# Sums of weight quarters by DMAs that add while landing, in the seven-product down-projection of one transformer block

## The chip, the cores and the metric

The kernel runs on one core of a Trainium2 chip. The metric is the device time of one execution in microseconds, median of 3 runs. PE is the matmul engine (TensorE), PEld its weight loads, DVE is VectorE, ACT is ScalarE, POOL is GpSimd and SP is SyncE, which here only issues DMAs.

## What is computed

One block of a network with 512 positions and 2048 columns: attention of two kinds, then a feed-forward part. The change touches the last product of the feed-forward part:

```
h = rmsnorm(x, g_ffn_pre[l])
u = causal_depthwise_conv(h @ w_up[l], conv_w[l], conv_b[l])
gate, val = jnp.split(u, 2, axis=-1)
y = (jax.nn.gelu(gate, approximate=True) * val) @ w_down[l]
x = x + rmsnorm(y, g_ffn_post[l])
```

`w_up` is 2048 x 11264, `w_down` 5632 x 2048, all float32.

## The kernel before

**Splitting.** A float32 operand is split into two parts that TensorE can take: `hi`, which ACT makes by a cast, and `lo`, which DVE makes as operand minus `hi`. A product is three matmuls: hi x hi, hi x lo, lo x hi. For weights `w_parts` does this (L797 to L803): the cast is L800, tile `wh`, and the subtraction L802, tile `wl`. Both tiles have three buffers, so a split can be done at most two products ahead of the one that PE is at.

**Seven products.** Both feed-forward products are done by blocks of two by two with seven block products instead of eight. `sevenfold` (L809) makes the seven weight operands from four quarters w11, w12, w21, w22 of a block of weights: three of them are w11 + w12, w11 + w12 + w22 and w11 + w12 + w22 + w21, formed one from another in w11's own buffer, and one is w12 + w22, formed in w12's. The sums are made on DVE by `plus` (L805, L806, tile `wr`). The other side has seven operands too: g11, g5, g6, g7, g12, g3, g22.

**Down-projection.** The gelu output lies in memory in units (`g_dram`). Four units make a chunk (`FU = 4`), and there are five chunks. `g_sides` (L967) loads a chunk (L970, tile `gr`, 2 MiB) and makes the seven operands from it: casts on ACT (L964), subtractions on DVE (L965), and differences in place on DVE (L974, L976, L977, L981). For each chunk there are two groups, q = 0 and 1, of 512 of the 1024 columns of each half; each does seven products. So the stage has ten groups. `down_steps` (L994) loads a quarter, 1 MiB in 512 rows of 2 KB, from SP (L999; four buffers), and `down_product` (L983, matmuls L991) does 24 matmuls for a product. `add_to` moves the results from PSUM into accumulators (ACT L958 in the first chunk, DVE L960 afterwards).

**What sets the order.** The program makes the weight operand of a step two steps before its product is issued (the loop at the end of the function). A scheduler of the language then sets the order on each engine and picks the buffers; each engine and each queue runs its instructions in that order. The order of the products is m1, m5, m6, m7, m2, m3, m4, so the sides are used in the order g11, g5, g6, g7, g12, g3, g22. m1 and m2 share a PSUM bank pair (X), m5 and m3 another (D), m7 and m4 a third (C).

Of the kernel before, what the change touches and what calls it, by code (L numbers as in the profile page):

```python
# [9 lines left out]
F32 = mybir.dt.float32  # L10
# [4 lines left out]
ALU = mybir.AluOpType  # L15
# [4 lines left out]
P = 128  # L20
S = 512
NT = S // P
# [27 lines left out]
def hymba_block(ctx, tc, x, xT, positions, vecs, taps, w_in, w_uq, w_ukv, w_o, g_attn_post, w_up, w_down,  # L50
                g_ffn_post, out):
    nc = tc.nc
    te, ve, sc, po, sy = nc.tensor, nc.vector, nc.scalar, nc.gpsimd, nc.sync

    const = ctx.enter_context(tc.tile_pool(name="const", bufs=1))
    sm = ctx.enter_context(tc.tile_pool(name="sm", bufs=8))
# [11 lines left out]
    def bank():  # L68
        return pp.tile([P, 512], F32, tag="ps", name="ps")

    def f(t):
        return t.bitcast(F32)
# [40 lines left out]
        te.matmul(ps, ll, rh, start=False, stop=stop)  # L113

    def rstd_of(ss, n):
        m = sm.tile([P, NT], F32, tag="ms", name="ms")
        ve.tensor_scalar(m, ss, 1.0 / n, EPS, ALU.mult, ALU.add)
        r = sm.tile([P, NT], F32, tag="rs", name="rs", bufs=8)
        po.tensor_tensor(r, m, nhalf, ALU.pow)
        return r  # L120
# [433 lines left out]
    def mla_scores(hd):  # L554
        e = hd % 2
        (qh, ql), (kh, kl) = q_mla.pop(hd), k_mla.pop(hd)
        hs = slice(64 * e, 64 * e + 64)
        qr = rope_q[hd // 2][e]
        regs = all_scores([(qh, kh), (qh, kl), (ql, kh), (qr, krh), (qr[hs], krl[hs])], mlamask)
        mx = sm.tile([P, NT], F32, tag="mx", name="mx", bufs=2)  # L560
        for b, (z, c0, c1) in enumerate(regs):
            ve.tensor_reduce(mx[:, b:b + 1], z[:, c0:c1], AX.X, ALU.max)
        nb = sm.tile([P, NT], F32, tag="nb", name="nb", bufs=2)
        ve.tensor_tensor(nb, mx, nsq, ALU.mult)
        den = sm.tile([P, NT], F32, tag="den", name="den", bufs=2)
        p = [page(("om", "s")[e], 3) for _ in range(3)]
        for b, (z, c0, c1) in enumerate(regs):
            sc.activation(p[min(b, 2)][:, c0:c1], z[:, c0:c1], AF.Exp, bias=nb[:, b:b + 1], scale=sq_[:, b:b + 1],
                          accum_out=den[:, b:b + 1])
        rden = sm.tile([P, NT], F32, tag="rden", name="rden", bufs=2)  # L570
        ve.reciprocal(rden, den)
        for b, (z, c0, c1) in enumerate(regs):
            pt = p[min(b, 2)][:, c0:c1]
            po.tensor_scalar(pt, pt, rden[:, b:b + 1], 1.0, ALU.mult, ALU.mult)
        return aget(*p)
# [34 lines left out]
    a = {0: mla_scores(0), 1: mla_scores(1)}  # L610
# [111 lines left out]
    def cpage(name):  # L722
        return cp.tile([P, 8, 256], R32, name=name)

    a5, a6, a3 = ((cpage(n + "h"), cpage(n + "l")) for n in ("a5", "a6", "a3"))
    lo_half, hi_half = slice(0, 256), slice(256, 512)
    a11, a12 = ((act_hi[:, k, lo_half], act_lo[:, k, lo_half]) for k in (slice(0, 8), slice(8, 16)))
    a7, a22 = ((act_hi[:, k, hi_half], act_lo[:, k, hi_half]) for k in (slice(0, 8), slice(8, 16)))
# [68 lines left out]
    def w_parts(w):  # L797
        n, cols = w.shape[1], w.shape[2]
        hi = wq.tile([P, n, cols], R32, tag="wh", name="wh", bufs=3)
        sc.copy(hi, w)  # L800
        lo = wq.tile([P, n, cols], R32, tag="wl", name="wl", bufs=3)
        ve.tensor_tensor(lo, w, f(hi), ALU.subtract)  # L802
        return hi, lo  # L803

    def plus(w, v):  # L805
        ve.tensor_tensor(w, w, v, ALU.add)  # L806
        return w

    def sevenfold(quarter):  # L809

        def q(*a):
            w = quarter(*a)
            return w

        w = {}

        def p1():
            w[11] = q(0, 0)
            return w_parts(w[11])

        def p5():
            w[12] = q(0, 1)
            return w_parts(plus(w[11], w[12]))

        def p6():
            w[22] = q(1, 1)
            return w_parts(plus(w[11], w[22]))

        def p7():
            return w_parts(plus(w[12], w[22]))  # L830

        def p2():
            w[21] = q(1, 0)
            return w_parts(w[21])

        def p3():
            return w_parts(w[22])

        def p4():
            return w_parts(plus(w[11], w[21]))  # L840

        return p1, p5, p6, p7, p2, p3, p4
# [96 lines left out]
    FU = 4  # L939
# [4 lines left out]
    def open_down():  # L944
        some(len(later))
        for st in (tp_stack, cp_stack, hp_stack):
            st.close()
        d["ap"], ap_ = stacked("ap")
        d["lp"], d["lpool"] = stacked("lp")
        d["gp"], d["gpool"] = stacked("gp")  # L950
        d["acc"] = {n: {(t, q): ap_.tile([P, S], F32, name=f"acc{n}{t}{q}") for t in range(2) for q in range(2)}
                    for n in ("11", "u2", "22", "21", "12")}

    def add_to(n, q, bs, first, op=ALU.add):
        for t in range(2):
            a = d["acc"][n][t, q]
            if first:
                sc.copy(a, bs[t])  # L958
            else:
                ve.tensor_tensor(a, a, bs[t], op)  # L960
# [31 lines left out]
                              stop=k == FU - 1 and i == 2, skip_group_check=True)  # L992

    def down_steps(ch, q):  # L994
        def quarter(kh, nh):
            w = wq.tile([P, FU, S], F32, tag="wr", name="wr", bufs=4)
            c0 = nh * 1024 + q * 512
            rows = w_down[ch * FU * 2 * P:(ch + 1) * FU * 2 * P, c0:c0 + 512]
            sy.dma_start(w, rows.rearrange("(k j p) c -> p k j c", p=P, j=2)[:, :, kh, :])  # L999
            return w  # L1000

        first = ch == 0
        z = {}

        def m1(w):
            if q == 0:
                if first:
                    open_down()
                d["g"] = g_sides(ch)
            z["X"] = [bank(), bank()]  # L1010
            down_product(z["X"], w, d["g"][1], True)
            add_to("u2", q, z["X"], first)

        def m5(w):
            z["D"] = [bank(), bank()]
            down_product(z["D"], w, d["g"][5], True)
            add_to("22", q, z["D"], first)

        def m6(w):
            Y = [bank(), bank()]  # L1020
            down_product(Y, w, d["g"][6], True)
            add_to("u2", q, Y, False, ALU.subtract)

        def m7(w):
            z["C"] = [bank(), bank()]
            down_product(z["C"], w, d["g"][7], True)
            add_to("22", q, z["C"], False, ALU.subtract)

        def m2(w):
            down_product(z["X"], w, d["g"][2], False)  # L1030
            add_to("11", q, z["X"], first)

        def m3(w):
            down_product(z["D"], w, d["g"][3], False)
            add_to("12", q, z["D"], first)

        def m4(w):
            down_product(z["C"], w, d["g"][4], False)
            add_to("21", q, z["C"], first)

        return zip(sevenfold(quarter), (m1, m5, m6, m7, m2, m3, m4))

    y = {}

# [97 lines left out]
    for make, use in stream():  # L1142
        queue.append((use, make()))
        if len(queue) > 2:
            use, w = queue.pop(0)
# [59 lines left out]
```

## Time and profile before

| | us |
|---|---|
| median of 3 runs | 2146.44 (2141.97 to 2148.74) |
| the profiled execution | 2146.34 |
| its span, first to last instruction | 2144.6 |
| PE busy | 2037.9 (95%) |
| DVE busy | 1583.2 (74%) |
| ACT busy | 944.1 (44%) |
| POOL busy | 122.3 (6%) |

The profile is of one execution. Busy time is the time in which an engine runs an instruction; idle time is written beside the instruction that ended it, with what it waited for. The granted clock (PEclk) is the share of its full speed, 2.4 GHz, at which PE was let run in a stretch. The DMA share is the mean busy share of the sixteen DMA engines.

### The profile page before, as it was taken

Reading aid. Unit: us, or ns where it says so; the run is one execution under the profiler, and the core shown is the slowest. Engines: PE = TensorE matmul, PEld = TensorE weight load, DVE = VectorE, ACT = ScalarE, POOL = GpSimd, SP = SyncE. Lnnn points to the kernel's source line nnn. Section 1 sums busy time; section 2 is a strip of 40 time slices with the busy share of each in tenths; the row PEclk is TensorE's granted clock in tenths of the full one; section 3 lists DMA queues with packets and bytes.
Section 4 is the critical chain, followed back from the end, with each engine's and each line's share of the span. In section 5 each row is a group of like instructions: output and inputs, shape, how many; then the busy total and the mean of one; then the engine's idle time right before and its main releaser. Section 6 shows DMA issues by size and latency. Waiting matters only on the chain.

```text
span 2144.6 us, 30034 instructions
## 1 busy us (share of the span) xinstructions
PE 2037.9 (95%) x12784; PEld 1819.6 (85%) x12784; DVE 1583.2 (74%) x1491; ACT 944.1 (44%) x1124; POOL 122.3 (6%) x147
## 2 busy tenths in 40 slices
PE   8999999999999569999999999999997999999996
PEld 6788788877888569999999999999997778778785
DVE  7355355776233679989889889889889788999985
ACT  6243234455323854544444444444444543343332
POOL 0000001122021200000000000000000000000004
PEclk9999999999999779999999999999998999999998
DMA  8322322211422342342342432432434344324252
GB/s 273 98 71 77 98 76 63 76 33 60 143 93 79 118 150 96 110 156 90 126 140 89 139 127 89 155 111 96 155 105 147 128 138 138 118 79 160 96 175 99
DMA packets 179062, 245.16 MB, mean 114 GB/s; under 512 B 8176, under 2 KB 127088, under 8 KB 178928
## 3 DMA queue, kind: packets, MB, share of 16 engines
q1 hardware_dynamic: 174048, 227.04, 32.9%
q0 software_dynamic: 4448, 15.73, 1.8%
q8 instruction: 100, 1.64, 0.3%
q10 hardware_dynamic: 432, 0.47, 0.1%
q14 instruction: 34, 0.28, 0.0%
HBM read 223.29 MB, written 19.92 MB: 113 GB/s over the span
## 4 chain that ended last, share of the span: by engine, by line
PE 84%; DVE 8%; ACT 3%; DMA 2%; issue 1%; POOL 0%; DVEq 0%; ACTq 0%; POOLq 0%
PE ps L858 40%; PE ps L991 15%; PE ps L111 8%; PE ps L112 8%; PE ps L113 8%; PE ps L258 2%; DVE wr L806 1%; DVE wl L802 1%; DMA wr<-in_w_in_dram 1%; PE ps L234 1%; ACT wh L800 1%; DVE x L1094 1%; DVE t L438 1%; DVE wl L107 0%; ACT wh L105 0%
## 5 line engine op out<-in xcount | busy, mean ns | idle before, releaser
L800 ACT CAST wh<-wr 128x2048 fp32r<-128x2048 f32 x228 | 435.1, 1912 | 575.1 <-DVE wr L806 227.2
L802 DVE TENSOR_TENSOR wl<-wr,wh 128x2048 fp32r<-128x2048 f32 x228 | 519.1, 2288 | 111.5 <-ACT wh L800 111.1
L858 PE MATMUL ps<-act_hi,wh 128*128 128x256 f32 x1408 | 395.5, 281 | 15.0 <-ACT wh L800 15.0
L858 PE MATMUL ps<-act_hi,wl 128*128 128x256 f32 x1408 | 394.1, 280 | 1.5 <-DVE wl L802 1.5
L858 PE MATMUL ps<-act_lo,wh 128*128 128x256 f32 x1408 | 393.9, 280 | 0.0
L806 DVE TENSOR_TENSOR wr<-wr 128x2048 f32<-128x2048 f32 x128 | 292.6, 2286 | 1.3
L107 DVE TENSOR_TENSOR wl<-wr,wh 128x1024 fp32r<-128x1024 f32 (+2 forms) x105 | 128.1, 1220 | 210.4 <-ACT wh L105 210.3
L858 PEld LDWEIGHTS ps<-act_hi,wh 128*128 128x128 f32 x1408 | 265.5, 189 | 15.4 <-ACT wh L800 15.4
L858 PEld LDWEIGHTS ps<-act_hi,wl 128*128 128x128 f32 x1408 | 265.8, 189 | 1.8 <-DVE wl L802 1.8
L858 PEld LDWEIGHTS ps<-act_lo,wh 128*128 128x128 f32 x1408 | 264.5, 188 | 0.0
L105 ACT CAST wh<-wr 128x1024 fp32r<-128x1024 f32 (+2 forms) x105 | 108.0, 1028 | 234.3 <-PE ps L112 98.9
L111 PE MATMUL ps<-wh,act_hi 128*128 128x512 f32 (+1 forms) x448 | 163.9, 366 | 8.0 <-ACT act_hi L182 6.7
L112 PE MATMUL ps<-wl,act_hi 128*128 128x512 f32 (+1 forms) x448 | 163.3, 365 | 1.7 <-DVE wl L107 1.6
L113 PE MATMUL ps<-wh,act_lo 128*128 128x512 f32 (+1 forms) x448 | 162.9, 364 | 0.0
L111 PE MATMUL ps<-act_hi,wh 128*128 128x512 f32 x368 | 146.8, 399 | 0.0
L112 PE MATMUL ps<-act_lo,wh 128*128 128x512 f32 x368 | 145.7, 396 | 0.0
L113 PE MATMUL ps<-act_hi,wl 128*128 128x512 f32 x368 | 144.6, 393 | 0.0
L111 PEld LDWEIGHTS ps<-wh,act_hi 128*128 128x128 f32 x448 | 84.9, 190 | 22.6 <-ACT act_hi L182 6.7
L112 PEld LDWEIGHTS ps<-wl,act_hi 128*128 128x128 f32 x448 | 85.2, 190 | 16.9 <-DVE wl L107 2.4
L858 PE MATMUL ps<-a3h,wh 128*128 128x256 f32 x352 | 98.6, 280 | 0.0
L858 PE MATMUL ps<-a6h,wh 128*128 128x256 f32 x352 | 98.5, 280 | 0.0
L858 PE MATMUL ps<-a5h,wh 128*128 128x256 f32 x352 | 98.5, 280 | 0.0
(315 smaller groups left out, 4337.9 us busy)
## 6 DMA issues: line engine op xcount, KB each, us to landing
wr<-in_w_up_dram SPq DMA_DIRECT2D x88, 1024.0 KB, 5.4
wr<-in_w_down_dram SPq DMA_DIRECT2D x44, 1024.0 KB, 6.2
wr<-in_w_in_dram SPq DMA_DIRECT2D x59, 512.0 KB, 3.7
wr<-in_w_o_dram SPq DMA_DIRECT2D x32, 512.0 KB, 3.5
g_dram<-bg POOLq DMA_DIRECT2D x22, 512.0 KB, 5.2
gr<-g_dram SPq DMA_DIRECT2D x5, 2048.0 KB, 9.9
acc<-in_x_dram SPq DMA_DIRECT2D x16, 256.0 KB, 4.7
x<-in_x_dram SPq DMA_DIRECT2D x16, 256.0 KB, 5.4
```

Source lines behind the costliest of these rows:

```text
L105: sc.copy(hi, raw)
L107: ve.tensor_tensor(lo, raw, f(hi), ALU.subtract)
L111: te.matmul(ps, lh, rh, start=start, stop=False)
L112: te.matmul(ps, lh, rl, start=False, stop=False)
L113: te.matmul(ps, ll, rh, start=False, stop=stop)
L234: te.transpose(dst, a(b, j), ident)
L258: te.matmul(dst, q[:, b * P:(b + 1) * P], k[:, k0:S], start=i == 0, stop=False)
L800: sc.copy(hi, w)
L802: ve.tensor_tensor(lo, w, f(hi), ALU.subtract)
L806: ve.tensor_tensor(w, w, v, ALU.add)
L858: te.matmul(dst, l[:, k, ms], r[:, k, :], start=fresh and k == 0 and m == 0 and i == 0, stop=k == 7 and i == 2, skip_group_check=True)
L991: te.matmul(bs[t], l[:, k, ts_], r[:, k, :], start=fresh and k == 0 and i == 0, stop=k == FU - 1 and i == 2, skip_group_check=True)
```

## The change

In the down-projection, the four sums of a group are no longer made by DVE. GpSimd issues a DMA that reads the quarter to be added from memory and adds it to the buffer that already holds the other (`added`, with `accum_op`). w12 gets w22 added as soon as it has landed; w11 gets w12, w22 and w21 added in turn, each after ACT and DVE have split what was there before. SP still loads four quarters a group, and GpSimd issues four adds of 1 MiB each beside it. The products come in the order m1, m2, m5, m7, m6, m3, m4, so that between two products with w11's buffer another one lies. The up-projection keeps its sums on DVE. The memory for DMA descriptors grows from 1024 to 2048 bytes a partition, and one small tile gets 4 buffers instead of 8.

```diff
-        m = sm.tile([P, NT], F32, tag="ms", name="ms")
+        m = sm.tile([P, NT], F32, tag="ms", name="ms", bufs=4)
...
-    def sevenfold(quarter):
-
-        def q(*a):
-            w = quarter(*a)
-            return w
+    def sevenfold(quarter, added=None):
 
         w = {}
+        q = quarter
+
+        def a1():
+            w[11] = q(0, 0)
+            parts = w_parts(w[11])
+            w[12] = q(0, 1)
+            added(w[12], 1, 1)
+            added(w[11], 0, 1)
+            return parts
+
+        def a2():
+            w[21] = q(1, 0)
+            return w_parts(w[21])
+
+        def a5():
+            parts = w_parts(w[11])
+            added(w[11], 1, 1)
+            return parts
+
+        def a7():
+            return w_parts(w[12])
+
+        def a6():
+            parts = w_parts(w[11])
+            added(w[11], 1, 0)
+            return parts
+
+        def a3():
+            w[22] = q(1, 1)
+            return w_parts(w[22])
+
+        def a4():
+            return w_parts(w[11])
+
+        if added:
+            return a1, a2, a5, a7, a6, a3, a4
...
     def down_steps(ch, q):
+        def rows(kh, nh):
+            c0 = nh * 1024 + q * 512
+            r = w_down[ch * FU * 2 * P:(ch + 1) * FU * 2 * P, c0:c0 + 512]
+            return r.rearrange("(k j p) c -> p k j c", p=P, j=2)[:, :, kh, :]
+
         def quarter(kh, nh):
             w = wq.tile([P, FU, S], F32, tag="wr", name="wr", bufs=4)
...
+            sy.dma_start(w, rows(kh, nh))
             return w
+
+        def added(w, kh, nh):
+            po.dma_start(w, rows(kh, nh), accum_op=ALU.add)
...
-        return zip(sevenfold(quarter), (m1, m5, m6, m7, m2, m3, m4))
+        return zip(sevenfold(quarter, added), (m1, m2, m5, m7, m6, m3, m4))
...
-    nc = bacc.Bacc("TRN2", target_bir_lowering=False, num_devices=1, dynamic_dma_scratch_size=1024)
+    nc = bacc.Bacc("TRN2", target_bir_lowering=False, num_devices=1, dynamic_dma_scratch_size=2048)
```

What the change makes of the engines' order stands here at three places, all in the third chunk. First ACT, the casts of the weights in the group q = 1, with the last cast of the group ahead. Before (w11 is wr_16328, w12 wr_16360, w21 wr_16461, w22 wr_16393; wr_16064 is w11 of the group ahead):

```order
L800 CAST wh_16298<-wr_16064 128x2048
L800 CAST wh_16330<-wr_16328 128x2048
L800 CAST wh_16363<-wr_16328 128x2048
L964 CAST g11h_16632<-gr_16630 128x1024
L800 CAST wh_16396<-wr_16328 128x2048
L800 CAST wh_16429<-wr_16360 128x2048
L800 CAST wh_16463<-wr_16461 128x2048
L800 CAST wh_16495<-wr_16393 128x2048
L800 CAST wh_16528<-wr_16328 128x2048
```

Now (w11 is wr_16328, w21 wr_16364, w12 wr_16334, w22 wr_16492):

```order
L800 CAST wh_16296<-wr_16064 128x2048
L800 CAST wh_16330<-wr_16328 128x2048
L800 CAST wh_16366<-wr_16364 128x2048
L800 CAST wh_16396<-wr_16328 128x2048
L996 CAST g11h_16633<-gr_16631 128x1024
L800 CAST wh_16429<-wr_16334 128x2048
L996 CAST g12h_16656<-gr_16631 128x1024
L800 CAST wh_16459<-wr_16328 128x2048
L800 CAST wh_16494<-wr_16492 128x2048
L800 CAST wh_16526<-wr_16328 128x2048
```

The second cast of w11 has moved behind that of w21, and the third behind that of w12; the first still follows the last of the group ahead.

Second, the sums of a group: before on DVE, in the group q = 0 of that chunk (L806), between splits and accumulations:

```order
L806 TENSOR_TENSOR wr_16064<-wr_16064,wr_16096 128x2048
L806 TENSOR_TENSOR wr_16096<-wr_16096,wr_16129 128x2048
L802 TENSOR_TENSOR wl_16101<-wr_16064,wh_16099 128x2048
L960 TENSOR_TENSOR acc2101_15141<-acc2101_15141,ps_16005 128x512
L960 TENSOR_TENSOR acc2111_15143<-acc2111_15143,ps_16006 128x512
L806 TENSOR_TENSOR wr_16064<-wr_16064,wr_16129 128x2048
L965 TENSOR_TENSOR g22l_16143<-gr_16136,g22h_16142 128x1024
```

Now on POOL's queue, from the group q = 0 (w11 is wr_16064) to the next chunk's (w12 wr_16564, w11 wr_16558):

```order
L1038 DMA wr_16064<-in_w_down_dram 128x4x512 x3
L1038 DMA wr_16334<-in_w_down_dram 128x4x512
L1038 DMA wr_16328<-in_w_down_dram 128x4x512 x2
L1038 DMA wr_16564<-in_w_down_dram 128x4x512
L1038 DMA wr_16328<-in_w_down_dram 128x4x512
L1038 DMA wr_16558<-in_w_down_dram 128x4x512 x3
```

The sums have left DVE; on POOL the third add of w11 stands behind the add of the next group's w12.

Third, PE at the start of the chunk, after the last matmul with g11. Before, the products follow each other:

```order
L991 MATMUL ps_16171<-wh_16066,g11l_16139 128x512
L991 MATMUL ps_16203<-wh_16099,g5h_16147 128x512
L991 MATMUL ps_16203<-wl_16101,g5h_16147 128x512
L991 MATMUL ps_16204<-wh_16099,g5h_16147 128x512
L991 MATMUL ps_16203<-wh_16099,g5l_16148 128x512
```

Now (wh_16132 is the split of w11 after its first add, wh_16102 that of w21):

```order
L1023 MATMUL ps_16172<-wh_16066,g11l_16140 128x512
L1023 MATMUL ps_16234<-wh_16132,g5h_16148 128x512
L1023 MATMUL ps_16234<-wl_16134,g5h_16148 128x512
L1023 MATMUL ps_16235<-wh_16132,g5h_16148 128x512
...
L1023 MATMUL ps_16235<-wh_16132,g5l_16149 128x512
L1023 MATMUL ps_16171<-wh_16102,g12h_16162 128x512
L1023 MATMUL ps_16171<-wl_16104,g12h_16162 128x512
```

Here 12 matmuls of g5 stand ahead of the first of g12; in the groups q = 1 it is one.

## Rows read from the trace of the kernel before

**Rows 1.** The page: busy us, share of the span, instructions.

```profile
PE 2037.9 (95%) x12784; PEld 1819.6 (85%) x12784; DVE 1583.2 (74%) x1491; ACT 944.1 (44%) x1124; POOL 122.3 (6%) x147
```

**Rows 2.** Windows of the down-projection: us, busy by engine, clock, DMA share, GB/s.

```profile
core 0: us, PE busy (x) PEld busy (x) DVE busy (x) ACT busy (x) POOL busy (x), PEclk, DMA share, GB/s
1657.30:2082.90 425.60, 405.56 (x1680) 322.55 (x1681) 381.99 (x293) 176.59 (x124) 0.53 (x1) 0.96 0.38 127
1826.30:1872.80 46.50, 42.04 (x170) 33.10 (x168) 43.36 (x35) 18.38 (x12) 0.00 (x0) 0.93 0.41 136
1872.80:1912.00 39.20, 39.20 (x170) 31.58 (x168) 35.85 (x28) 15.22 (x10) 0.00 (x0) 1.00 0.34 108
1912.00:1958.30 46.30, 41.84 (x169) 32.98 (x168) 43.35 (x35) 18.38 (x12) 0.00 (x0) 0.93 0.41 137
```

**Rows 3.** Timeline of PE: start us, us, instruction, [idle before <-releaser].

```profile
1657.31 0.79 PE L991 MATMUL ps<-wh,g11h 128*128 128x512 f32 x1 [12.65 <-ACT g11h L964]
...
1826.30 0.39 PE L991 MATMUL ps<-wh,g11h 128*128 128x512 f32 x1
...
1836.53 0.80 PE L991 MATMUL ps<-wh,g5h 128*128 128x512 f32 x1 [4.46 <-ACT g5h L964]
...
1872.80 0.40 PE L991 MATMUL ps<-wh,g11h 128*128 128x512 f32 x1
...
2082.92 0.40 PE L111 MATMUL ps<-wh,glh 128*128 128x512 f32 x1
```

**Rows 4.** Chain of waits through a chunk start: start us, us, what.

```profile
1823.83 2.29 DVE wr L806
1826.12 2.20 DVE wl L802
1829.52 2.21 DVE wr L806
1836.53 64.22 PE ps L991 x263
```

**Rows 5.** Timeline of ACT at that chunk start.

```profile
1826.27 1.06 ACT L964 CAST g22h<-gr 128x1024 fp32r<-128x1024 f32 x1 [0.45 <-PE ps L991]
...
1835.43 1.04 ACT L964 CAST g5h<-gr 128x1024 fp32r<-128x1024 f32 x1
```

**Rows 6.** Groups of the stage (1657 to 2083): busy us, mean ns, idle before.

```profile
L806 DVE TENSOR_TENSOR wr<-wr 128x2048 f32<-128x2048 f32 x37 | 84.6, 2287 | 0.4
```

**Rows 7.** DMA issues: engine, count, KB each, median us from issue to landing.

```profile
wr<-in_w_down_dram SPq DMA_DIRECT2D x44, 1024.0 KB, 6.2
...
g_dram<-bg POOLq DMA_DIRECT2D x22, 512.0 KB, 5.2
...
x_dram<-x POOLq DMA_DIRECT2D x16, 256.0 KB, 3.1
...
out_dram<-x SPq DMA_DIRECT2D x16, 256.0 KB, 2.4
...
gl<-g_dram SPq DMA_DIRECT2D x2, 512.0 KB, 3.3
```

**Rows 8.** Timelines of ACT and DVE: one weight split.

```profile
1850.64 1.91 ACT L800 CAST wh<-wr 128x2048 fp32r<-128x2048 f32 x1 [3.69 <-PE ps L991]
...
1852.58 2.29 DVE L802 TENSOR_TENSOR wl<-wr,wh 128x2048 fp32r<-128x2048 f32 x1 [0.45 <-ACT wh L800]
```

**Rows 9.** Timeline of POOL: the last store of g_dram.

```profile
1658.91 0.53 POOL L932 DMA_DIRECT2D g_dram<-bg  x1 [34.62 <-DVE bg L931]
```

More of the change, by code (lines that the diff above doesn't have):

```diff
@@ L994, in down_steps @@
     def down_steps(ch, q):
+        def rows(kh, nh):
+            c0 = nh * 1024 + q * 512
+            r = w_down[ch * FU * 2 * P:(ch + 1) * FU * 2 * P, c0:c0 + 512]
+            return r.rearrange("(k j p) c -> p k j c", p=P, j=2)[:, :, kh, :]
         def quarter(kh, nh):
             w = wq.tile([P, FU, S], F32, tag="wr", name="wr", bufs=4)
-            c0 = nh * 1024 + q * 512
-            rows = w_down[ch * FU * 2 * P:(ch + 1) * FU * 2 * P, c0:c0 + 512]
-            sy.dma_start(w, rows.rearrange("(k j p) c -> p k j c", p=P, j=2)[:, :, kh, :])
-            return w
+            sy.dma_start(w, rows(kh, nh))
+            return w
+        def added(w, kh, nh):
+            po.dma_start(w, rows(kh, nh), accum_op=ALU.add)
         first = ch == 0
```

## Prediction

> **What bounds the kernel now.** The page's first part comes first [rows 1]: TensorE (PE) is busy 95% of the span, VectorE (DVE) 74%, GpSimd (POOL) 6%. Such means hide the stage that the change touches, so the windows come next [rows 2]. The first line of them is the whole down-projection stage: 425.60 us for ten groups of seven products, PE busy 405.56, DVE 381.99 (90%). The other lines are single groups. A group inside a chunk takes 39.20 us with PE busy for all of it, and seven products of 5.6 us make it up. A group that opens a chunk takes 46.50 or 46.30, at a granted clock of 0.93 instead of 1.00. So PE sets the pace but for the chunk starts, and only the surplus over 10 x 39.2 = 392 us, that is 33.6 us, can be won here. It lies in five chunk starts: 7.3 and 7.1 in the two shown, and the others are alike.
>
> PE's rows show where [rows 3]. At 1836.53 the first product with g5 waited 4.46 us for ACT's cast of g5; the very first product waited 12.65 us for g11, ahead of this window. The chain of waits [rows 4] says why g5 is late: ahead of each such start stand DVE's sums (wr, L806) and splits (wl, L802), each 2.2 to 2.3 us, and behind them g5. ACT had cast g22 at 1826.27, but g5 at 1835.43 [rows 5].
>
> **What the change does, part by part.**
>
> *DVE's sums go.* 40 of them (four a group), each 2287 ns [rows 6] (37 in the stage, three just ahead), are 91.5 us of DVE work. Beside PE's work they cost nothing, so what they return is the chunk starts: with them gone, and with m2 between m1 and m5 so that g5 is needed later, up to 7.2 us at four starts, 28.8 us. The 12.65 us at the very start stay, since the load of gr and the casts behind it stay.
>
> *40 adds by DMA come.* Each brings 1 MiB from memory and adds it to a buffer; GpSimd issues them, and in the stage it has only one busy instruction now, of 0.53 us [rows 2]. No row shows such a DMA, so I bound the time L from its issue to its landing. Lower end: a plain 1 MiB load of the same weight takes 6.2 us [rows 7]; nothing of it is saved by adding, so no less. Two terms may come on top.
> First, the buffer's old content must be fetched too, one more MiB through the same DMA engines. In the group from 1872.80 the engines were busy 0.34 x 39.20 = 13.3 us for four such loads (108 GB/s x 39.2 us = 4.2 MB) [rows 2], so 3.3 us per MiB. The term is 0 if both fetches overlap, 3.3 if they queue. I take 3.3, since the engines are what both share.
> The Trainium skill, "Collectives: The Full Stack", Part 3 ("Why ReduceScatter is half of AllGather"), says that an add inside the DMA engines needs two source reads, both on one read ring, and so halves the rate. By it the transfer doubles; without it, with fetches that overlap fully, the sum below would be 2146.3 - 11.6 = about 2135. No run here shows it yet.
> Second, GpSimd's queue instead of SyncE's. For 512 KB, POOL's store took 5.2 us and SP's load 3.3; for 256 KB POOL's store 3.1, SP's 2.4 [rows 7]: 1.9 and 0.7 more, for 128 runs of memory each. An add has 512 runs, so the ends are 0.7 and 4 x 1.9 = 7.6. I take 1.3, the middle of the two pairs as they stand.
> L = 6.2 + 3.3 + 1.3 = 10.8 us; ends 6.9 and 17.1, and 6.2 if the queue costs nothing.
>
> *The chain.* w11's buffer is split four times in a group, with an add between each two. A split is ACT's cast, 1.91 us from 1850.64, and DVE's subtraction, from 1852.58 for 2.29: 4.2 us together [rows 8]. The ACT rows above show the next group's first cast right behind the last cast of this one; both are in program order, so the chain of one group hangs on the end of the last: 4.2 for the last split, 2.3 for the subtraction of the next group's first, an add, 4.2, an add, 4.2, an add. That is 14.9 + 3L. Before, three 2.3 us sums stood where the adds are: 14.9 + 6.9 = 21.8 us, under the 39.2 of PE, hence no wait.
> The adds also meet other traffic: in a period of some 51 us four plain loads (13.2 us) and w12's add (6.6) fill 39% of the engines' time, so a link whose extra is shared by halves is stretched by about 0.39 x 3.3 = 1.3 us, and three links by 4. Ends: 0, and twice that.
> Period: 14.9 + 32.4 + 4 = 51.3 us, 12.1 over PE's 39.2. Ten groups: 513 us, against 425.6 now: +87.4. The 28.8 us of the chunk starts are not taken off again, for the chain and no longer g5 ends the wait there; as long as PE waits for the chain, DVE's relief is worth nothing.
>
> *The new product order.* Between two splits of w11 now lie two products, 11.2 us, and a split can be done up to two products ahead of its use. But PE's built order puts 1 to 12 matmuls of g5 ahead of g12's, so PE waits for the first add's split one product earlier than the list of products says. As the chain is a cycle, this shifts the wait, and doesn't lengthen it: 0. Behind the waiting cast of w11, ACT holds g11's, g12's or g5's casts, and their matmuls wait anyway.
>
> *Queues.* POOL is in order, and the third add stands behind the next group's w12 add, which needs its own load (6.2 us) after a7's split. That load starts one split behind a5's, so the w12 add is issued before add 2 has landed: 0, beyond the sharing above. The last store of g_dram stands behind three adds; the three are out before its data, which came at 1658.91 [rows 9]: 0, or some us at the first chunk. SP keeps its 44 loads; gr, which would be the next to be late, is loaded nearly a chunk ahead. The pool of ms halves for five uses far apart, and the larger DMA scratch is memory only: 0 both.
>
> **Sum.** The profiled execution took 2146.34 us (span 2144.6; within 0.1 us of the median of the three runs, 2146.44). 2146.3 + 87.4 = 2233.7; I say 2234.
>
> **Rivals.**
> *A. The add costs about what a load costs.* At L = 6.2 the period is 14.9 + 18.6 + 4 = 37.5, under 39.2: PE sets the pace, the chunk starts close, and the time is 2146.3 - 28.8 = 2118. It turns at L = 6.8, (39.2 - 18.9) / 3. For it: the engines are busy 38% of the stage [rows 2], so a second fetch has room. Against it: latency counts here, not room, and every POOL row is slower than its SP row. 18%.
> *B. A draw.* At L = 7.9 the period is 42.6, the stage's mean now: 2146. 8%.
> *C. GpSimd's queue is the bound.* If its cost grows with the runs, 4 x 0.7 to 4 x 1.9, then L = 12.3 to 17.1. Between, at L = 13.7, the period is 60, the stage 600, the time 2321; at 17.1 it is 70.2 and 2423. For it: four times the runs, and more to write for each. Against it: POOL has nothing else to do, and the next descriptors could be written while the last drain. 17%.
> *D. The spacing doesn't take place*, since PE's order has g5 first. It would matter only with L near 7 to 8, where it makes B out of A; it is in B's share.
> The forecast, L from 8.5 to 12.5, has 57%; its own range is 2165 to 2285.
>
> **How the numbers follow.** A measurement of this kernel tells about 0.3%, 6.4 us. Faster is A, 18%; the same is B, 8%; slower is the forecast and C, 74%. The range for 8 in 10 goes from 2125, which leaves out the better third of A, to 2320, which leaves out half of C.
>
> **What would show it.** Right: 40 POOL issues of about 10.8 us to landing; ACT's casts of w11 waiting for a DMA, no longer for DVE's sums; PE waiting in every group for ACT's wh, a period near 51 us, PE busy near 77% and a granted clock under 1.00 in all groups; DVE's share down by 91.5 us of work. The adding step is wrong if adds land within 7 us, and the queue step if they take over 13. The chain step is wrong if L is 10.8 and groups still take 40 us, which would mean that the next group's first split isn't tied to the last; or if they take 60, which would mean that loads and adds block each other on a queue. If every group is at 39.2 with g5 no longer waited for, A holds.

## The result and the profile after

The changed kernel takes 2232.96 us, the median of 4 runs (2231.81 to 2263.95); the kernel before took 2145.51 beside it (2141.97 to 2148.74). The ratio is 1.0443, with a 95% interval of 1.0352 to 1.0534. It is slower, and the time is within 1.1 us of the forecast of 2234. The sum behind the forecast is not as good as that looks: three parts of it were off, by 14.6, 13.5 and 28.8 us, and that the first two cancel the third is luck. The profiled execution took 2233.21 us with a span of 2231.3. Single executions of one program, of the kernel before too, fell some 30 us off its others (2263.95 here), which is why the interval is wide.

The first part of its page, beside [rows 1]: DVE is down by 90.3 us (91.5 were forecast), POOL up by 51.5.

```profile
PE 2035.2 (91%) x12784; PEld 1805.1 (81%) x12784; DVE 1492.9 (67%) x1451; ACT 944.2 (42%) x1124; POOL 173.8 (8%) x187
```

The windows, beside [rows 2]: the whole stage, then a group q = 1 and a group q = 0 (the columns are those of [rows 2]).

```profile
1642.07:2169.63 527.56, 434.26 (x1680) 340.96 (x1681) 296.91 (x253) 173.66 (x124) 48.14 (x38) 0.88 0.73 172
1797.00:1856.00 59.00, 42.79 (x168) 33.60 (x167) 26.80 (x24) 15.01 (x9) 6.12 (x5) 0.86 0.68 150
1856.07:1903.48 47.41, 41.30 (x170) 32.59 (x168) 34.35 (x30) 18.05 (x12) 3.86 (x3) 0.96 0.84 208
```

The stage grew from 425.60 to 527.56, by 102.0 us. Its groups take 47.1 to 49.1 us at q = 0 and 58.6 to 59.5 at q = 1, but for the last, which took 50.3. PE's timeline shows both kinds of wait, and a larger one ahead of the stage. Beside [rows 3], where g11 was waited for 12.65 us and g5 4.46:

```profile
1642.07 0.80 PE L1023 MATMUL ps<-wh,g11h 128*128 128x512 f32 x1 [26.19 <-ACT g11h L996]
...
1811.86 0.79 PE L1023 MATMUL ps<-wh,g5h 128*128 128x512 f32 x1 [9.58 <-ACT wh L800]
...
1846.78 0.49 PE L1023 MATMUL ps<-wh,g22h 128*128 128x512 f32 x1 [2.67 <-ACT wh L800]
```

So PE now waits for the cast of a sum that a DMA makes. Nearly all of these waits, 52.0 us in ten, lie in the groups q = 1. At the starts of the second to the fifth chunk PE still waits 3.0 to 3.9 us for g5, but g5's cast now stands right behind such a cast. For the second chunk, on ACT:

```profile
1755.86 1.90 ACT L800 CAST wh<-wr 128x2048 fp32r<-128x2048 f32 x1 [4.77 <-DMA wr<-in_w_down_dram]
1757.67 1.04 ACT L996 CAST g5h<-gr 128x1024 fp32r<-128x1024 f32 x1
```

and on PE:

```profile
1758.76 0.79 PE L1023 MATMUL ps<-wh,g5h 128*128 128x512 f32 x1 [3.43 <-ACT g5h L996]
```

Waiting is not all of the 102.0 us: PE is busy 434.26 us in the stage instead of 405.56, with the same matmuls at a granted clock of 0.88 instead of 0.96. The page's DMA issues, beside [rows 7], give the price of an add: an add lands 9.4 us after its issue, and SP's loads, with more traffic around them, take 7.6 instead of 6.2.

```profile
wr<-in_w_down_dram SPq DMA_DIRECT2D x44, 1024.0 KB, 7.6
wr<-in_w_down_dram POOLq DMA_DIRECT2D x40, 1024.0 KB, 9.4
```

**Where the 86.7 us between the spans lie.** The stage gives +102.0. The wait of 26.19 us ahead of it gives +13.5. Then 28.8 us are missing, and they lie in the up-projection, which the change doesn't touch: PE begins the wait 28.8 us earlier than before (1615.88 against 1644.66, from the stage's first product less its wait). 102.0 + 13.5 - 28.8 = 86.7; the tail is unchanged. The windows of 18 of the 22 units of the up-projection, from the second store of g_dram to the twentieth, show it. Before:

```profile
871.86:1584.18 712.32, 712.32 (x6050) 712.32 (x6049) 616.29 (x451) 326.66 (x253) 9.61 (x18) 1.00 0.37 120
```

After:

```profile
873.28:1558.99 685.71, 685.71 (x6053) 685.71 (x6052) 615.04 (x452) 329.23 (x252) 9.61 (x19) 1.00 0.38 125
```

PE is busy all the time in both, at a granted clock of 1.00 in both, with the same matmuls (a few records apart). One takes 712.32 / 6050 = 117.7 ns before and 113.3 after.

**One group in detail.** POOL's timeline from the w12 add of a group q = 1 (1787.17) to the first w11 add of the next (1852.86). The brackets hold the idle time before and its releaser; "issue" means that the profile shows nothing waited for.

```profile
1787.17 1.29 POOL L1038 DMA_DIRECT2D wr<-in_w_down_dram  x1 [8.38 <-issue]
1796.69 1.28 POOL L1038 DMA_DIRECT2D wr<-in_w_down_dram  x1 [8.24 <-issue]
1814.54 1.29 POOL L1038 DMA_DIRECT2D wr<-in_w_down_dram  x1 [16.56 <-DVE wl L802]
1826.76 1.28 POOL L1038 DMA_DIRECT2D wr<-in_w_down_dram  x1 [10.93 <-DMA wr<-in_w_down_dram]
1835.89 1.29 POOL L1038 DMA_DIRECT2D wr<-in_w_down_dram  x1 [7.85 <-issue]
1852.86 1.28 POOL L1038 DMA_DIRECT2D wr<-in_w_down_dram  x1 [15.69 <-DVE wl L802]
```

ACT's casts of w11 after each add:

```profile
1809.91 1.90 ACT L800 CAST wh<-wr 128x2048 fp32r<-128x2048 f32 x1 [17.45 <-DMA wr<-in_w_down_dram]
...
1823.66 1.91 ACT L800 CAST wh<-wr 128x2048 fp32r<-128x2048 f32 x1 [0.45 <-DMA wr<-in_w_down_dram]
...
1844.83 5.50 ACT L800 CAST wh<-wr 128x2048 fp32r<-128x2048 f32 x3 [15.26 <-DMA wr<-in_w_down_dram]
```

DVE's subtraction behind the second:

```profile
1825.60 2.29 DVE L802 TENSOR_TENSOR wl<-wr,wh 128x2048 fp32r<-128x2048 f32 x1 [1.13 <-ACT wh L800]
```

An add's way from its issue to the cast takes 13.2 us for the first (1796.69 to 1809.91), 9.1 for the second and 8.9 for the third. The third could be issued when the subtraction ends, at 1827.89; it is issued at 1835.89, 8.0 us later, behind the next group's w12 add of 1826.76, and POOL is neither busy nor waiting for an engine. The cycle of 56.2 us is 31.2 of adds, 14.9 of splits, 8.0 of this wait and some 2 us between.

### The profile page after: what moved, and what is told of

Same layout as the page of the kernel before. It is cut to its first block, busy times and chain, and to the rows that moved or that the text cites. A ratio compares the mean times of both kernels' runs of the same rounds, so it can differ in the third digit from the quotient of the medians.

```text
span 2231.3 us, 30108 instructions
## 1 busy us (share of the span) xinstructions
PE 2035.2 (91%) x12784; PEld 1805.1 (81%) x12784; DVE 1492.9 (67%) x1451; ACT 944.2 (42%) x1124; POOL 173.8 (8%) x187
## 5 line engine op out<-in xcount | busy, mean ns | idle before, releaser
L890 PE MATMUL ps<-act_hi,wh 128*128 128x256 f32 x1408 | 390.1, 277 | 15.4 <-ACT wh L800 15.4
L806 DVE TENSOR_TENSOR wr<-wr 128x2048 f32<-128x2048 f32 x88 | 201.1, 2286 | 0.9
L890 PE MATMUL ps<-a5l,wh 128*128 128x256 f32 x352 | 97.2, 276 | 0.0
L890 PE MATMUL ps<-a5h,wl 128*128 128x256 f32 x352 | 97.2, 276 | 0.0
```

Of the source, the lines that this page charges most:

```text
L890: te.matmul(dst, l[:, k, ms], r[:, k, :], start=fresh and k == 0 and m == 0 and i == 0, stop=k == 7 and i == 2, skip_group_check=True)
```

## The experiments

The rate of the up-projection's matmuls differs between programs, and some 30 us of the time with it, so each run is read by three numbers of its profile beside its time: a unit of the up-projection (spacing of the stores of g_dram), PE's wait ahead of the stage, and the stage (first product with g11 to the first of the tail). e6_links, e8_one, e9_two and e10_oldorder were run once, the others several times; the numbers in the table are of one profiled execution each.

| run | sums by DMA | order | up unit | start wait | stage |
|---|---|---|---|---|---|
| before | none | old | 39.57 | 12.65 | 425.6 |
| changed | all four | new | 38.08 | 26.19 | 527.6 |
| e1_scratch | none | old | 38.08 | 13.10 | 418.8 |
| e2_order | none | new | 39.57 | 10.54 | 424.1 |
| e4_ring | all four | new | 40.32 | 14.61 | 498.8 |
| e5_plain | (plain loads) | new | 38.08 | 14.16 | 425.1 |
| e6_links | w11's three | new | 38.08 | 15.02 | 474.4 |
| e8_one | w11's first | new | 39.57 | 11.73 | 442.2 |
| e9_two | w11's first two | new | 38.08 | 11.84 | 427.4 |
| e10_oldorder | all four | old | 38.08 | 33.71 | 551.0 |
| e11_shift | none | old | 38.08 | 13.10 | 421.6 |
| e3_order_scratch | none | new | 38.08 | 12.63 | 414.0 |
| e7_w12 | w12's | new | 38.08 | 12.88 | 405.6 |
| e12_room_place | all four | new | 39.57 | 14.27 | 497.6 |

The larger descriptor memory and the smaller ms, which the change brings along, act on the stage too: e1_scratch has them alone, and its stage is 6.8 us shorter than before (e11_shift's, 4.0). What the adds cost is therefore read best against e3_order_scratch, which has everything of the change but them: 113.6 us in the stage, 13.6 ahead of it, and 125 us in all (2232.96 against 2107.81).

**What an add costs by itself: e5_plain.** The changed kernel with each add as a plain load into the same buffer; it leaves out the sums, so its output is not the product:

```diff
-            po.dma_start(w, rows(kh, nh), accum_op=ALU.add)
+            po.dma_start(w, rows(kh, nh))
```

> The changed kernel with the 40 adds issued as plain loads into the same buffers by the same queue in the same order (the sums are left out: a buffer holds only the last quarter that landed). It prices the fetch of the buffer's old content. Theory 'second fetch': issue to landing falls from 9.4 us by about 3.3, to 6 to 6.5, the period of a group falls by three times that, and the stage to about 430; total 2135 or so. Rival 'queue': the price lies in GpSimd's queue and its 512 runs of memory, then landing stays within 1 us of 9.4 and the stage within 30 us of 527.6.

Measured: 2115.3 us, the median of four runs (2112.17 to 2147.14). Its DMA issues:

```profile
wr<-in_w_down_dram SPq DMA_DIRECT2D x44, 1024.0 KB, 6.5
wr<-in_w_down_dram POOLq DMA_DIRECT2D x40, 1024.0 KB, 7.0
```

The same loads on the same queue land after 7.0 us, the adds after 9.4: adding costs 2.4 us of latency. GpSimd's queue costs a plain load 0.5 us over SP's beside it. The 2.4 us are not the second fetch alone, for an add is also written as more descriptors: GpSimd is busy 1.29 us for an add and 0.75 for a plain load. The pages show it for the queue that GpSimd's DMAs use (packets, MB, their time as a share of 16 engines' span); first the changed kernel, then e5_plain:

```profile
q0 software_dynamic: 25568, 57.68, 13.0%
```

```profile
q0 software_dynamic: 15328, 57.68, 8.0%
```

Less the 4448 packets and 1.8% that this queue has without any of them (the kernel before), an add is 528 packets and a plain load 272, for the same bytes. The same shares give the time: an add keeps the sixteen engines busy for 6.3 us (13.0% of 2231.3 less 1.8% of 2144.6, over 40), a plain load for 3.3.

The stage is 425.1, 102 us shorter than with the adds, though the 40 transfers, the order of waits and the descriptor memory are those of the changed kernel. But it is 11.1 us longer than e3_order_scratch's. And the run takes away two things at once: the longer landing, and the waits with no releaser on POOL, of which it has none. What these are, and that they are worth 30 us, stands under e12_room_place.

**The order alone, and the order under the adds: e2_order and e10_oldorder.** The first keeps the new order and makes the sums on DVE (with the old descriptor memory); the second keeps the adds and puts the old order back. Of the changed kernel, in e2_order, where w11's other two sums change likewise:

```diff
-            parts = w_parts(w[11])
-            added(w[11], 1, 1)
-            return parts
+            w[12] = q(0, 1)
+            return w_parts(plus(w[11], w[12]))
...
-            return w_parts(w[12])
+            w[22] = q(1, 1)
+            return w_parts(plus(w[12], w[22]))
...
```

and in e10_oldorder:

```diff
-            return a1, a2, a5, a7, a6, a3, a4
+            return a1, a5, a6, a7, a2, a3, a4
...
-        return zip(sevenfold(quarter, added), (m1, m2, m5, m7, m6, m3, m4))
+        return zip(sevenfold(quarter, added), (m1, m5, m6, m7, m2, m3, m4))
```

> The kernel before with the new order of the products alone: sums by DVE, scratch as before. Theory 'order': g5 is needed one product later, so the four chunk starts close: the down-projection stage (first product with g11 to the last operand of the tail) goes from 425.6 us to about 400, the total to about 2120 at the old up-projection rate or 2087 at the fast one. Rival 'DVE': the sums in DVE's queue keep g5 late and the order alone does nothing: stage within 5 us of 425.6.

> The changed kernel with all 40 adds by DMA and the products in the old order m1, m5, m6, m7, m2, m3, m4, where three products with w11's buffer follow each other. Theory 'chain': the chain is a cycle from one group's last split to the next one's first, and the order of the products only moves the waits: stage within 25 us of 527.6. Rival 'spacing': each add is needed one product earlier and every link waits 5.6 us more, stage about 527.6 + 10 x 2 x 5.6 = 640.

Measured: 2142.73 us for the order alone, against 2147.38 of before (medians of 10 and 13 runs; nine of the ten took 2140.21 to 2147.05, one 2106.45), 1.5 us of it in the stage. So the order alone does next to nothing, as the rival had it. The old order under the adds took 2261.48, in one run. Its stage:

```profile
1647.37:2198.35 550.98, 433.72 (x1680) 341.50 (x1681) 305.09 (x255) 174.36 (x124) 47.55 (x37) 0.87 0.70 167
```

That is 23.4 us over the changed kernel's 527.56, inside the 25 of the theory, and the start wait is 7.5 more. So the new order is worth 31 us under the adds, by this one run, and little where DVE makes the sums (1.5 us of the stage here, 4.8 from e1_scratch to e3_order_scratch). The 23.4 us lie at the chunk starts: the groups that open the second to the fifth chunk take 53.1 to 55.6 us instead of 47.1 to 49.1, and in them PE waits 7.9 to 11.3 us for g5 instead of 3.0 to 3.9. In the old order the product with g5 is the second of the group:

```profile
1764.94 0.80 PE L1023 MATMUL ps<-wh,g5h 128*128 128x512 f32 x1 [11.28 <-ACT g5h L996]
```

**How many links: e6_links, e8_one, e9_two.** Some of the adds go back to DVE's `plus`. Of the changed kernel, in e6_links:

```diff
-            w[12] = q(0, 1)
-            added(w[12], 1, 1)
...
-            return w_parts(w[12])
+            w[12] = q(0, 1)
+            w[22] = q(1, 1)
+            return w_parts(plus(w[12], w[22]))
...
-            w[22] = q(1, 1)
```

e9_two also makes the last sum of w11 on DVE, e8_one the last two.

> The changed kernel with the sum of w12 and w22 made by DVE again; the three adds into w11's buffer stay DMAs (30 adds in all). Theory 'chain': the three adds, each waiting for the split ahead of it, set the period at 14.9 + 3 x 9.4 + 4 = 47 us, and no add has another in front of it any more, so POOL's waits without releaser go and the stage (first product with g11 to the tail's first) is 465 to 485 us. Rival 'traffic': the loss of 102 us goes with the bytes, a quarter of them is gone, stage about 502.

> The changed kernel with one add by DMA a group, the first of w11's chain, the other three sums by DVE; new order of products. Theory 'chain': 14.9 + 2 x 2.3 + 9.4 + 1.3 = 30 us is under PE's 39, so nothing is lost, and the chunk starts stay eased: stage 385 to 410 us. Rival 'traffic': a quarter of the loss stays, stage about 450.

> The changed kernel with two adds by DMA a group, the first and second of w11's chain, the other two sums by DVE. Theory 'chain': 14.9 + 2.3 + 2 x 9.4 + 2.7 = 39 us, about PE's own pace: stage 390 to 425 us. Rival 'traffic': half of the loss stays, stage about 475.

Measured, in one run each: 2168.14, 2161.50 and 2116.95 us. The up unit of e8_one is 39.57, so its total is some 33 us too long to be compared with the other two; the stages can be. With w11's three adds and no w12 add:

```profile
1630.86:2105.27 474.41, 422.60 (x1681) 334.65 (x1682) 315.05 (x259) 174.12 (x124) 36.14 (x28) 0.92 0.69 170
```

This is 53.2 us under the changed kernel: ten adds that are no link of the chain cost over half of what the stage lost. Leaving out w11's last add as well saves 47.0 more and brings the stage to 427.4. One add instead of two saves nothing: 442.2, where 385 to 410 was expected. Its matmuls ran at the slower rate, but that is some 7 us of it (e1_scratch against before); what else holds this stage was not found. So from three adds to two the stage follows the chain, and below that something else than the chain sets it.

**Room for descriptors: e4_ring.** The changed kernel with 64 bytes a partition more for them:

```diff
-    nc = bacc.Bacc("TRN2", target_bir_lowering=False, num_devices=1, dynamic_dma_scratch_size=2048)
+    nc = bacc.Bacc("TRN2", target_bir_lowering=False, num_devices=1, dynamic_dma_scratch_size=2112)
```

> The changed kernel with 2112 instead of 2048 bytes of DMA scratch, nothing else. In the profile after, POOL stood still ten times, 85.3 us in all, with no releaser shown, each time right behind an add. Theory 'room': an add's descriptors fill more than half of the scratch, so the next add cannot be written until the one ahead has drained; with room for two these waits go, the groups q = 1 fall from 58.6 to about 51 us and the stage from 527.6 to about 490, total about 2195. Rival 'traffic': the DMA engines are what is short (busy 0.73 of the stage), the waits move into the landing time: stage within 8 us of 527.6.

Measured: four runs from 2230.06 to 2235.27 us, ratio 1.0399 (1.0383 to 1.0414): no gain over the changed kernel's total. Yet the stage is 28.8 us shorter and the start wait 11.6. The gain was lost in the up-projection, whose 18 units took 726.03 us at a clock of 1.00, 119.9 ns a matmul:

```profile
865.86:1591.89 726.03, 726.03 (x6053) 726.03 (x6052) 616.53 (x451) 326.54 (x253) 9.61 (x19) 1.00 0.36 118
```

**The place of the tiles: e1_scratch and e11_shift.** The first is the kernel before with the change's two memory edits alone; the second has an unused tile in place of the larger descriptor memory, so that all other tiles lie where e1_scratch has them. Of the kernel before, in e1_scratch:

```diff
-        m = sm.tile([P, NT], F32, tag="ms", name="ms")
+        m = sm.tile([P, NT], F32, tag="ms", name="ms", bufs=4)
...
-    nc = bacc.Bacc("TRN2", target_bir_lowering=False, num_devices=1, dynamic_dma_scratch_size=1024)
+    nc = bacc.Bacc("TRN2", target_bir_lowering=False, num_devices=1, dynamic_dma_scratch_size=2048)
```

and in e11_shift, with ms as above:

```diff
+    pad = const.tile([P, 256], F32, name="pad")
+    po.memset(pad[:, 0:1], 0.0)
```

> The kernel before with the larger DMA scratch (2048 bytes) and four buffers of ms alone; sums and order as before. It asks why the up-projection, which the change does not touch, took 38.08 us a unit in the profile after and 39.57 before (22 units, 33 us). Theory 'places': the tiles lie at other addresses, and that makes every matmul 4.5 ns shorter there; then all runs come to about 2146 - 33 = 2113 us and the unit takes 38.08 us. Rival 'draw': PE comes out of an idle time at one of two rates, whatever the addresses; then runs come near 2146 or near 2113, not all near one of them, or all stay at 2146.

> The kernel before with an unused tile of 1024 bytes a partition put ahead of all others, and 4 buffers of ms, so that every tile lies where it lies in the changed kernel, and the memory for descriptors stays at 1024 bytes. Nothing else is changed. Theory (the place of the operands decides at which of two rates the up-projection's matmuls run): a unit of 38.08 us instead of 39.57 in most of its runs, so about 2111 us, as the run with the larger descriptor memory gave; single runs at 2145 may occur. Rival (the larger descriptor memory itself does it): units of 39.57 us and 2146 us in all runs.

Measured: ratios 0.9835 (0.9819 to 0.9851) and 0.9838 (0.9824 to 0.9851), 1.6% faster than the kernel before without a line of its work changed; the medians are 2111.86 and 2113.17. Both profiles have 38.08 us a unit. So it isn't the descriptor memory but the shift of the tiles by it. The place alone does not settle an execution, though: one of e1_scratch's four took 2143.99 us and one of e11_shift's five 2142.96, near the kernel before, so the rival of a draw holds in part.

**Room and place together: e12_room_place.** e4_ring with ms at 2 buffers, which puts the up-projection's operands back where the changed kernel has them.

```diff
-        m = sm.tile([P, NT], F32, tag="ms", name="ms", bufs=4)
+        m = sm.tile([P, NT], F32, tag="ms", name="ms", bufs=2)
...
-    nc = bacc.Bacc("TRN2", target_bir_lowering=False, num_devices=1, dynamic_dma_scratch_size=2048)
+    nc = bacc.Bacc("TRN2", target_bir_lowering=False, num_devices=1, dynamic_dma_scratch_size=2112)
```

> The changed kernel with 2112 bytes for descriptors, as in the run with room for two adds, and ms with 2 buffers, so that the up-projection's tiles lie again where they lie in the changed kernel. Theory (room for a second add gives the stage 29 us and its start 12 us back, and the run with 2112 bytes hid that only because its tiles lay elsewhere and the up-projection ran at 40.32 us a unit): units of 38.08, a stage of 499, a start wait of about 15, in all 2233 - 29 - 12 = 2192 us. Rival (the larger descriptor memory itself slows the up-projection, in whatever place): units near 40.32 and 2230 us.

Measured: 2192.50, 2196.19, 2196.72 and 2202.48 us, and 2224.25 for the profiled one; ratio 1.0277 (1.0160 to 1.0393). Four of five lie near the 2192 of the theory; only the fifth was profiled, so their rate is read from the time alone. The fifth has its own explanation in its profile: 18 units took 712.59 us, 117.7 ns a matmul, as in the kernel before.

```profile
876.40:1588.99 712.59, 712.59 (x6053) 712.59 (x6052) 616.60 (x451) 326.93 (x253) 9.58 (x18) 1.00 0.37 120
...
1663.58:2161.15 497.57, 425.90 (x1681) 335.26 (x1681) 295.20 (x250) 173.64 (x124) 47.54 (x37) 0.91 0.75 181
```

Room gave the stage 30.0 us and its start 11.9. The waits of POOL show by what. Changed kernel (line waited for, us in total, times, longest):

```profile
POOL wr L1038 <- DVE wl L802: 316.8, 21, 25.0
POOL wr L1038 <- issue: 85.3, 10, 10.1
POOL wr L1038 <- DMA wr<-in_w_down_dram: 65.4, 6, 16.0
```

With 2112 bytes:

```profile
POOL wr L1038 <- DVE wl L802: 400.7, 29, 23.6
POOL wr L1038 <- DMA wr<-in_w_down_dram: 51.4, 8, 11.1
...
POOL wr L1038 <- issue: 0.3, 1, 0.3
```

Ten waits of 8.5 us for nothing that the profile shows are gone. They were waits for room: in the changed kernel no two adds of the stage are issued less than 9.1 us apart, and with 2112 bytes nine pairs are issued less than 4 us apart, as here:

```profile
1839.01 1.29 POOL L1038 DMA_DIRECT2D wr<-in_w_down_dram  x1 [11.09 <-DMA wr<-in_w_down_dram]
1840.96 1.28 POOL L1038 DMA_DIRECT2D wr<-in_w_down_dram  x1 [0.66 <-DVE wl L802]
```

The plain loads of e5_plain, with half the packets, have room for two in the 2048 bytes: nine pairs of them are issued less than 5 us apart. Room is not all gain, since two adds then share the engines: the median add lands after 10.1 us instead of 9.4, and the slowest after 18.2.

**Versions that beat both: e3_order_scratch and e7_w12.** The new order with the change's memory edits and all sums on DVE (as e2_order), and the same with w12's sum alone by a DMA. Of e3_order_scratch, in e7_w12:

```diff
-            return w_parts(plus(w[11], w[12]))
+            parts = w_parts(plus(w[11], w[12]))
+            added(w[12], 1, 1)
+            return parts
...
-            w[22] = q(1, 1)
-            return w_parts(plus(w[12], w[22]))
+            return w_parts(w[12])
...
+            w[22] = q(1, 1)
```

> The new product order and the larger descriptor memory, but all four sums on DVE. Theory (the adds cost all that the stage lost, the order alone gives back 1 to 2 us of chunk starts, the lower rate of a matmul does the rest): a stage of 424 x 5.49 / 5.60 = 416 us, an up-projection unit of 38.08, some 2107 to 2111 us. Rival (the two gains do not add up, since the up-projection falls back to 39.57 a unit): about 2145 us.

> New order and larger descriptor memory, with only w12's sum by a DMA that adds (10 adds instead of 40) and w11's three sums on DVE. Theory (an add costs nothing where it is not a link of w11's chain and has the queue for itself): a stage of 416 to 420 us, 2107 to 2115 us. Rival (an add of 9 us is itself too late for the product with w12, or takes the plain loads' place): PE waits 2 to 5 us in each group, a stage of 435 to 465 us, 2127 to 2160 us.

Measured: e3_order_scratch 2107.81 us (2103.52 to 2136.73), ratio 0.9811 (0.9796 to 0.9826). e7_w12: 2094.38, 2095.77, 2130.09 and 2132.20 us; its lower pair is the lowest of all runs here, but two of four lie 36 us above, so no interval is given. Their stages, first e3_order_scratch:

```profile
1626.61:2040.62 414.01, 395.59 (x1681) 317.63 (x1682) 381.27 (x292) 176.03 (x124) 0.23 (x1) 0.98 0.39 130
```

and e7_w12:

```profile
1627.24:2032.85 405.61, 396.09 (x1680) 317.05 (x1681) 359.29 (x281) 176.20 (x124) 11.62 (x9) 0.99 0.53 153
```

At 405.6 the stage is 9.5 us above its 396.1 of PE work, and 8.4 under e3_order_scratch's: here the ten adds into w12 cost PE nothing and take 22 us off DVE. By the stage of one profile each, this is the one use of these DMAs here that pays. The same ten adds cost 53.2 us where the adds of w11 share the queue and the engines with them (e6_links): 30.0 of it is room (e12_room_place), and 23.2 is left.

## Why the prediction was right, and by which errors

The number came out by luck, the mechanism didn't: of the forecast's +87.4 the stage took 14.6 more, the start 13.5 that were put at about 0, and the up-projection gave back 28.8 that were put at 0.

**The mechanism** is as forecast: the chain through w11's buffer, four splits and three adds, sets the pace; ACT's `wh` waits for a DMA, and PE for `wh` in the groups q = 1 and, from the second chunk's start on, for a g5 cast behind such a `wh`; the stage's clock is 0.88. e6_links and e9_two show that the period follows the links as long as there are three of them. PE's share came out higher than the 77% forecast, 82%, since its matmuls take longer at that clock.

**The landing, L = 10.8: 9.4 measured.** The plain load (6.2) stood. The second fetch was put at 3.3; an add lands 2.4 later than a plain load (e5_plain), and some part of that, perhaps the 0.5 us that GpSimd is busy longer, is not the fetch. In time of the engines the 3.3 was near: 6.3 against 3.3 us, 3.0 more. The queue was put at 1.3, and is 0.5 for a plain load over SP's in the same run, or 0.8 over 6.2. The argument that "every POOL row is slower than its SP row" held for the pairs chosen only: on the same page SP's 256 KB load of x from x_dram took 6.1 us, and POOL's store of it 3.1. The rule of the Trainium skill that was weighed there ("Collectives: The Full Stack", Part 3, "Why ReduceScatter is half of AllGather") speaks of the rate of a long stream. The trace agrees with it in the engines' time, which about doubles (3.3 to 6.3 us), but the latency of one transfer grows by 34% (7.0 to 9.4) and doesn't double.

**The period, 51.3: 52.8 measured.** With L = 9.4 the chain is 14.9 + 28.2 = 43.1. Of the 9.7 us on top, room for descriptors is 3.0 (30.0 us by e12_room_place, over ten groups), and 6.7 is left where 4 were put for the sharing of the engines. Without the w12 adds the period is 47.4 = 14.9 + 27.9 + 4.6 (e6_links), and no wait for room is left in POOL's rows. With them and with room it is 49.8 = 14.9 + 30.3 + 4.6, the landing then being 10.1 (e12_room_place). So the 4 for sharing was near where adds needn't wait for room. In the changed kernel 3L was 4.2 too long, and what stands around it 5.7 too short.

**"Queues ... 0, beyond the sharing above" failed.** The step looked at what each DMA waits for and at the order of the queue, and not at whether two adds fit into the descriptor memory. They don't, and the third add stands 8.0 us behind the next group's w12 add. The same sentence of the forecast, on the third add, had the place right and the price wrong.

**"0, or some us at the first chunk" failed: 13.5.** In the changed kernel the first w12 add is issued at 1603.00, and w11's first add only at 1616.60, 7.4 us after DVE had split w11 (1609.16). It then takes 16.4 us to land, the longest of the 40. ACT's cast of that sum holds the queue until it lands, with the gelu work and g11's cast behind it:

```profile
1603.00 1.38 POOL L1038 DMA_DIRECT2D wr<-in_w_down_dram  x1 [5.65 <-DMA wr<-in_w_down_dram]
1616.60 1.30 POOL L1038 DMA_DIRECT2D wr<-in_w_down_dram  x1 [12.22 <-DVE bv L898]
```

```profile
1633.07 1.90 ACT L800 CAST wh<-wr 128x2048 fp32r<-128x2048 f32 x1 [19.37 <-DMA wr<-in_w_down_dram]
```

The forecast had looked at the last store behind these adds, but not at what stands behind the cast on ACT. With room the add goes out 0.6 us after the split (1642.73, split by 1642.15), the cast follows 10.5 us later at 1653.27, and the wait is 14.27 (e12_room_place). So room gave the start 6.8 us by the earlier issue and 6.0 by the quicker landing. The load of gr (2 MiB) is issued at 1616.62, together with the add, in the changed kernel and 7.3 us behind it in e12_room_place; that it slows the landing is likely, but was not tried apart. (The bracket at 1616.60 names an instruction of DVE that ended just then; it is not what the add needed.)

**"The larger DMA scratch is memory only: 0 both" failed: -28.8.** It moves the tiles, and the up-projection ran at 113.3 ns a matmul instead of 117.7. This is the error that hid the other two. Without it the time would have been 2233.2 + 28.8 = 2262, 28 over the forecast, still inside the range. The one execution of 2263.95 us lies there; it was not the profiled one, so that it ran at 117.7 ns is not shown.

**The new order, "0": half right.** It is worth 1.5 to 4.8 us of the stage without adds, and 31 in all under them (e10_oldorder, one run). "As the chain is a cycle, this shifts the wait, and doesn't lengthen it" holds for the groups q = 1, which take 56.3 to 59.7 us in the old order and 50.3 to 59.5 in the new, but not for the chunk starts: there PE's waits for g5 are 40.2 us in the old order and 16.1 in the new, and that difference is about the stage's 23.4. The start's 7.5 us were not followed up.

**The chunk starts**, 28.8 us that were not taken off, were rightly left: e5_plain has the sums off DVE, a chain of 14.9 + 21.0 = 35.9 us, less than PE's work, and still takes 42.5 a group, though PE waits only 2.5 us for g5 in its whole stage. Its other waits there are short and many (8.0 us for accumulations, 5.7 for `wl`, 2.4 for `wh`), and the stage's clock is 0.96; what stands behind them was not followed up. So **rival A's price was wrong**: near its turning point the stage gave nothing, and with a landing of 7.0 us it is as long as before. Rival C, the queue as the bound by its cost per run of memory, isn't borne out (0.5 us); the queue did cost, by another mechanism. Rival D did not take place: the built order has g5 first, and by e10_oldorder the new order helps all the same.

What stays open: why the place of the tiles changes the rate of a matmul, why single executions of one program have the other rate, and what holds the stage of e8_one.

## What to carry to other kernels

A DMA that adds while landing is no replacement for a vector add in a chain: it puts 9.4 us where 2.3 stood, and every link passes that on. Where a sum is off the chain and no other adds share its queue, the same DMA cost nothing and took work off the vector engine (e7_w12); beside the adds of the chain it cost 53.2 us (e6_links). Before judging a change by its total, compare a stage that it doesn't touch: here the untouched stage moved by 29 us, a third of the effect, and twice hid what the change did.

## What had not been expected of the hardware

The same up-projection, PE busy throughout at a granted clock of 1.00, ran at three rates: 113.3, 117.7 and 119.9 ns for a matmul of 256 columns (windows of 685.71, 712.32 and 726.03 us). Moving the tiles by 896 bytes (1024 of the unused tile less 128 of ms) changed which rate most executions have (e11_shift), and a program can have either (e12_room_place: 712.59 in the profiled execution, and four others some 28 us shorter in all).

POOL is busy 1.28 us for an add that lands after 9.4, and between, an add that finds no room for its descriptors waits without a releaser in the profile: idle time that ends by "issue" on a queue that has DMAs on their way is worth an experiment with the memory, which here gave back 30.0 us of the stage for 64 bytes a partition. The Trainium skill, "Perfetto Trace Analysis", "DMA Instruction — SWDGE (GPSIMD)", says that GpSimd's end of such an instruction is the writing of its last descriptor and not the end of the transfer, which these two numbers agree with.
